# Start-up loads on two queues, own blocks for six operand splits, and a longer period for the second stream of weight sums in a fused attention and feed-forward layer

## The chip, the cores and the metric

The kernel runs on one core of a Trainium2 chip, as one launch. The metric is the device time of one execution in microseconds (us); lower is better. The times of before are those of three runs: 1481.43, 1481.87 and 1482.26 us.

## The reference, cut to what matters

One layer on x of 256 rows and 2048 columns, in float32, with a memory `mem` of the same shape:

```python
proj = rms_norm(x, g_mix) @ w_in               # heads of three attentions, and 3 x 2048 gate columns
mk, mv = split(rms_norm(mem, g_mem) @ w_mem_kv, 2)
o_fox, o_sb, o_mem = forgetting(...), stick_breaking(...), memory(...)
g = sigmoid(gates + b_gate)
merged = g[0] * (o_fox @ w_br_fox) + g[1] * (o_sb @ w_br_sb) + g[2] * (o_mem @ w_br_mem)
x = x + merged @ w_out
u_gate, u_val = split(causal_conv3(rms_norm(x, g_ffn) @ w_up) + conv_b, 2)
return x + (silu(u_gate) * u_val) @ w_down
```

In the stick-breaking attention (six heads of width 128), with z the scaled scores, the weight of key j for query i is exp(log_sigmoid(z) + R), where R is the sum of log(1 - sigmoid(z)) over the keys between j and i. That sum is made by a matrix product with a triangle of ones.

## The kernel before, in words

Every large product is float32 work done in three passes. A float32 operand is split into a rounded part `hi` and a rest `lo`: `piece` (lines 134 to 145) loads a piece of a weight (1024 columns per partition) into one of four `raw` buffers with a DMA on SyncE's queue (SP), ScalarE (ACT) copies it to `hi` (line 140), VectorE (DVE) subtracts to get `lo` (line 141). TensorE (PE) then does hi times hi, lo times hi, hi times lo in `passes` (lines 147 to 153), three matmuls of 512 columns each. There are four `raw`, four `hi` and four `lo` buffers.

The work goes through PE in this order: the key and value product of the memory (`kv`, 16 steps of k, lines 450 to 485), the projections with w_in (mq, f0 to f4, s0 to s4, and twelve gate products g, in four column groups n), the three branch products b of each n, the output product o, the up product u with its convolution, and the down product.

**The start.** `memres` holds `mem`. The helper `mem_piece(k, n)` loads n column blocks of 128 from block k on, always on SP's queue (line 275). Block 0 is asked for first; then `kvw` block 0 as two halves of 512 columns, mem block 1, and in the loop over k the weight of k + 1 as one piece of 1024 columns (`kv_weights`) and mem blocks 2k + 2 and 2k + 3 for k under 7; from k = 7 on the x columns (`x_piece`, line 426). PE transposes mem blocks (line 192), ACT and DVE scale and split them into `memT` (lines 178 and 181), and `kv_part` (line 438) runs the two column halves of the step. Small constants (gains, tap rows of the convolution, a bias; lines 305 to 326) are issued on SP as well. They are a generator that advances once per step from k = 2 on, and they are not pinned: a scheduler that lays out each engine's instructions ahead of the run may move them. Instructions that go through `pin` or `in_order` keep their order among each other. Each DMA counts on one of eight completion semaphores in turn, so that a DMA waits at its issuing queue until the one eight places before it (of both queues) has landed.

**The blocks.** `block` takes one of 14 buffers of 1024 columns (`bp`); heads, gates and transposed products live in them. Small work goes through the pool `sm`; its tag `junk` has two buffers of 512 columns.

**The stick-breaking heads.** `sb_head` (line 651) is a generator; two heads are in work at a time, and each `tick()` (one per two k of a product) takes one step of each. A head computes log(1 - sigmoid) into `l1`, masks it with GpSimd (POOL, line 646), splits it into two parts `ls[0]` (ACT, line 669) and `ls[1]` (DVE, line 670), and multiplies these with the triangle (line 674) and the ones (line 676). Both parts are `junk` tiles, so one head's two parts fill both buffers until its matmuls have read them.

**The weight sums.** For 22 pairs of w_down's row blocks the down product uses sums of weights made beforehand. `weight_sums(staging, period)` takes 44 half pairs from one shared list. For each it loads 512 KB (two DMAs on SP, line 232), adds on DVE (lines 239 to 241), and five ticks later stores 512 KB (`kept`, line 244). A new half starts every `period` ticks. The first stream starts at the end of mq, has period 6, and stages in one buffer of its own (`pre`), so that its next load waits for the landing of its last store. The second starts at n = 1 with period 8 and stages in blocks. Both draw from the list until it is empty; all must be done by the end of the o product.

Of the kernel before, what the change touches and what calls it, by code (L numbers as in the profile page):

```python
# [10 lines left out]
F32R = mybir.dt.float32r  # L11
# [4 lines left out]
P = 128  # L16
# [24 lines left out]
def hybrid_block(  # L41
# [25 lines left out]
    nc = tc.nc  # L67
# [5 lines left out]
    sm = ctx.enter_context(tc.tile_pool(name="sm", bufs=4))  # L73
# [6 lines left out]
    def bank(name):  # L80
        return pp.tile([P, 512], F32, tag="bank", name=name)
# [14 lines left out]
    def later(gen):  # L96
        waiting.append(gen)

    background = []
# [28 lines left out]
    def pin(ins):  # L128

        if pinned[0]:  # L130
            tc.keep_in_program_order(ins)


    def piece(src, a, n, name):
        raw = wp.tile([P, PIECE], F32, tag="raw", name=f"raw_{name}")
        hi = wp.tile([P, PIECE], F32R, tag="hi", bufs=SBUFS, name=f"hi_{name}")
        lo = wp.tile([P, PIECE], F32R, tag="lo", bufs=SBUFS, name=f"lo_{name}")
        m = a * n
        pin(nc.sync.dma_start(raw[:, :m].rearrange("p (a n) -> p a n", a=a), src))
        pin(nc.scalar.copy(hi[:, :m], raw[:, :m]))  # L140
        pin(nc.vector.tensor_tensor(lo[:, :m], raw[:, :m], hi[:, :m].bitcast(F32), ALU.subtract))  # L141
        return (
            hi[:, :m].rearrange("p (a n) -> p a n", a=a),
            lo[:, :m].rearrange("p (a n) -> p a n", a=a),
        )
# [76 lines left out]
    def weight_sums(staging, period):  # L222

        while halves:
            nb, pr, h = halves.popleft()
            if h == 0:
                sums_of[nb, pr] = dram.tile([P, 4, 512], F32, tag=f"kept_{nb}_{pr}", name=f"kept_{nb}_{pr}")
            w = staging(f"pre_{nb}_{pr}_{h}").rearrange("p (i c) -> p i c", i=4)
            n0 = nb * PIECE + h * 256
            for n in range(2):  # L230
                in_order(
                    nc.sync.dma_start(
                        w.rearrange("p (k n) c -> p k n c", k=2)[:, :, n],
                        dv[:, 2 * pr : 2 * pr + 2, n0 + n * 512 : n0 + n * 512 + 256],
                    )
                )

            both = w[:, 1:2].to_broadcast([P, 2, 256])
            in_order(nc.vector.tensor_tensor(w[:, 0:2], w[:, 0:4:3], both, ALU.add))
            in_order(nc.vector.tensor_tensor(w[:, T2], w[:, T1], w[:, T2], ALU.add))  # L240
            in_order(nc.vector.tensor_tensor(w[:, T4], w[:, T2], w[:, T4], ALU.add))
            for _ in range(5):
                yield
            in_order(nc.sync.dma_start(sums_of[nb, pr][:, :, h * 256 : (h + 1) * 256], w))
            for _ in range(period - 5):
                yield
# [6 lines left out]
    mv = mem[0].rearrange("(t p) d -> p t d", p=P)  # L253
    memres = xt_pool.tile([P, NT, D], F32, tag="xt", name="memres")
# [16 lines left out]

    tiles_of = lambda g: g.rearrange("(k p) -> k p", p=P)

    def mem_piece(k, n=2):
        pin(nc.sync.dma_start(memres[:, :, k * P : (k + n) * P], mv[:, :, k * P : (k + n) * P]))

    rows_mem = load_rows(nc.scalar, [(tiles_of(g_mem[0]), KT)], "mem")
    mem_piece(0, 1)
    bfor = cst.tile([P, N_FOX], F32, name="bfor")

    ones_r = cst.tile([P, P], F32R, name="ones_r")
# [87 lines left out]
    def block(name, dt=F32):  # L369
        return bp.tile([P, 1024], dt, tag="blk", name=name)  # L370
# [64 lines left out]
    kv = [[bank(f"kv_{c}_{t}") for t in range(NT)] for c in range(2)]  # L435
    kvw = w_mem_kv[0].rearrange("(k p) n -> p k n", p=P)
# [7 lines left out]
    w = {}  # L444

    def kv_weights(k):
        wh, wl = piece(kvw[:, k : k + 1, :], 1, 1024, f"kv{k}")
        w[k] = [(wh[:, 0, c * 512 : (c + 1) * 512], wl[:, 0, c * 512 : (c + 1) * 512]) for c in range(2)]

    h0 = [piece(kvw[:, :1, :512], 1, 512, "kv0_0")]  # L450
    to_mT(0, 1)
    keep_busy(3)
    h0.append(piece(kvw[:, :1, 512:], 1, 512, "kv0_1"))
    w[0] = [(h[:, 0], l[:, 0]) for h, l in h0]
    mem_piece(1, 1)
    xT = None
    squares = deque((j, t) for j in range(4) for t in range(NT))
    for k in range(KT):
        if k == 0:
            kv_part(0, 0, *w[0][0])  # L460
            to_mT(1, 1)
        if k + 1 < KT:
            kv_weights(k + 1)
        if k < 7:
            mem_piece(2 * k + 2)
        elif k < 15:
            x_piece(2 * (k - 7))
        if k == 2:
            later(constants())
        if k > 0:  # L470
            kv_part(k, 0, *w[k][0])
        if 0 < k < 8:
            to_mT(2 * k)
        elif k > 8:
            transposed(xT, xres, gmix, 2 * (k - 9), "xT")
        kv_part(k, 1, *w.pop(k)[1])
        for _ in range(0 if k < 3 else 1 if k < 8 else 3):
            if squares:
                j, t = squares.popleft()
                square_part(ssm, memres, j, "m", (t,))  # L480
        if k == 8:
            row_rstd(rstd_m, ssm, "m")
            xT = k_tiles("xT")
        tick()
# [156 lines left out]
    W3 = 3 * P  # L641
# [9 lines left out]
    def sb_head(h):  # L651
        yield from until("s0", "s1", "s2")
        q, k = qs[h // 4][:, h % 4], qs[(N_SB + h) // 4][:, (N_SB + h) % 4]
        b = block(f"sb_{h}")
        lb, l1 = b[:, :W3], b[:, W3 : 2 * W3]
        Z = bank(f"z_{h}")
        z = Z[:, :W3]
        nc.tensor.matmul(z[:, :S], lhsT=k[:, :P], rhs=q, start=True, stop=True)
        nc.tensor.matmul(z[:, S:], lhsT=k[:, P:], rhs=q[:, P:], start=True, stop=True)
        nc.scalar.activation(lb, z, AF.Abs)  # L660
        nc.scalar.activation(lb, lb, AF.Exp, scale=-1.0)
        nc.scalar.activation(lb, lb, AF.Ln, bias=1.0)
        nc.vector.scalar_tensor_tensor(lb, z, 0.0, lb, ALU.min, ALU.subtract)
        nc.vector.tensor_tensor(l1, lb, z, ALU.subtract)
        diagonal(l1)
        yield 2

        ls = [sm.tile([P, 512], F32R, tag="junk", bufs=2, name=f"ls_{h}_{i}")[:, :W3] for i in range(2)]
        nc.scalar.copy(ls[0], l1)
        nc.vector.tensor_tensor(ls[1], l1, ls[0].bitcast(F32), ALU.subtract)  # L670
        yield 1
        r = bank(f"r_{h}")
        for i in range(2):
            nc.tensor.matmul(r[:, :W3], lhsT=after_r, rhs=ls[i], start=i == 0, stop=False)
        for i in range(2):
            nc.tensor.matmul(r[:, P:S], lhsT=ones_r, rhs=ls[i][:, S:], start=False, stop=i == 1)
        nc.vector.tensor_tensor(lb, lb, r[:, :W3], ALU.add)
        nc.scalar.activation(lb, lb, AF.Exp)
        diagonal(lb)
        yield 2  # L680
        yield from until("vs0", "vs1")
        weighted(lb, vs, h, N_FOX + h, Z)
# [31 lines left out]

    for n in range(4):
        if n == 1:
            background.append(weight_sums(block, 8))
        n0 = n * 512
        gate = []
        for b in range(3):  # L720
            bg = gp.tile([P, 512], F32, tag="bg", name=f"bg_{n}_{b}")
            nc.sync.dma_start(bg, b_gate[0, b, n0 : n0 + 512].partition_broadcast(P))
            ps = proj(C_GATE + b * D + n0, 512, f"g{n}_{b}")
            g = rows_of(block(f"g_{n}_{b}"))
            for t in range(NT):
                nc.vector.scalar_tensor_tensor(g[:, t], ps[t], rstd[:, t : t + 1], bg, ALU.mult, ALU.add)
            if n > 0:
                nc.scalar.activation(g, g, AF.Sigmoid)
            gate.append(g)
        if n == 0:  # L730
            finish()
            for g in gate:
                in_order(nc.scalar.activation(g, g, AF.Sigmoid))
        acc = rows_of(block(f"acc_{n}"))
        for i, (w, k0, nk, b) in enumerate(branches):
            ps = product(lambda k: oT[:, k0 + k], w[0], nk, n0, 512, f"b{n}_{b}")
            for t in range(NT):
                g = gate[b]
                if i == 0:
                    nc.vector.tensor_tensor(acc[:, t], g[:, t], ps[t], ALU.mult)  # L740
                else:
                    nc.vector.tensor_tensor(g[:, t], g[:, t], ps[t], ALU.mult)
                    nc.vector.tensor_tensor(acc[:, t], acc[:, t], g[:, t], ALU.add)
        later(merged_T(acc, n))
# [22 lines left out]
    for n in range(4):  # L767
        c = slice(n * 512, (n + 1) * 512)
# [48 lines left out]
    for f0 in range(0, FT, 4):  # L817
        for s in range(2):
            ps = [bank(f"u{f0 + i}_{s}") for i in range(4)]
            c0 = s * D_FF + f0 * P  # L820
            for k in range(0, KT, 2):
                hi, lo = piece(upv[:, k : k + 2, c0 : c0 + 512], 2, 512, f"u{f0}_{s}_{k}")
                for j in range(2):
                    first, last = k + j == 0, k + j == KT - 1
                    for i in range(4):
                        c = slice(i * P, (i + 1) * P)
# [167 lines left out]
    for nb, plan in enumerate(plans):  # L994
# [17 lines left out]
        for t in range(NT):  # L1012
            for n in range(2):
                c = n0 + n * 512
                o = xres[:, t, c : c + 512]
                nc.vector.tensor_tensor(o, o, X[t][n], ALU.add)
                if (nb, t, n) == (1, 1, 1):
                    nc.scalar.dma_start(ov[:, t, c : c + 256], o[:, :256])
                    c, o = c + 256, o[:, 256:]
# [35 lines left out]
```

## Time and profile before

| what | value |
|---|---|
| median of 3 runs | 1481.87 us (1481.43 to 1482.26) |
| the profiled execution's own time | 1483.94 us |
| its span, first to last instruction | 1482.2 us |
| DVE busy | 1073.0 us (72%) |
| ACT busy | 801.8 us (54%) |
| HBM read, written | 320.60 MB, 25.17 MB |
| granted TensorE clock | 0.999 |

The span leaves 1.74 us of the profiled execution's own time outside it. The profile's busy time of PE is the time in which some matmul is under way; matmuls overlap, and their ends are modelled. Waits are named by the engine that waited, the line, and whom it waited for. In a timeline row stand the start, the length, the engine (SPq and ACTq are the queues that issue DMAs), the line, the operation, the tiles written and read, their shape, a count, and in brackets the idle time of the engine before it with what ended it.

### The profile page before, as it was taken

Reading aid. Unit: us, or ns where it says so; the run is one execution under the profiler, and the core shown is the slowest. Engines: PE = TensorE matmul, PEld = TensorE weight load, DVE = VectorE, ACT = ScalarE, POOL = GpSimd, SP = SyncE. Lnnn points to the kernel's source line nnn. Section 1 sums busy time; section 2 is a strip of 40 time slices with the busy share of each in tenths; the row PEclk is TensorE's granted clock in tenths of the full one; section 3 lists DMA queues with packets and bytes.
Section 4 is the critical chain, followed back from the end, with each engine's and each line's share of the span. In section 5 each row is a group of like instructions: output and inputs, shape, how many; then the busy total and the mean of one; then the engine's idle time right before and its main releaser. Section 6 shows DMA issues by size and latency. Waiting matters only on the chain.

```text
span 1482.2 us, 20334 instructions
## 1 busy us (share of the span) xinstructions
PE 1473.9 (99%) x7394; PEld 1248.5 (84%) x7394; DVE 1073.0 (72%) x1604; ACT 801.8 (54%) x1141; POOL 17.9 (1%) x46
## 2 busy tenths in 40 slices
PE   9999999999999999999999999999999999999999
PEld 6888888888888887888888888888888888888887
DVE  5777676666765867666557787787787787997877
ACT  6755454464544343444456565565565565674664
POOL 0000000011000000000000000000000000000000
PEclk9999999999999999999999999999999999999999
DMA  9686687587788989975556566556556656798796
GB/s 306 197 276 208 189 290 222 172 274 233 260 288 282 322 290 306 313 252 191 184 180 207 187 187 198 185 185 198 188 186 195 189 184 203 242 318 280 248 338 216
DMA packets 198308, 347.12 MB, mean 234 GB/s; under 512 B 12458, under 2 KB 66622, under 8 KB 198206
## 3 DMA queue, kind: packets, MB, share of 16 engines
q1 hardware_dynamic: 196878, 343.71, 71.4%
q10 hardware_dynamic: 1328, 2.11, 0.4%
q8 instruction: 58, 0.95, 0.2%
q14 instruction: 44, 0.36, 0.1%
HBM read 320.60 MB, written 25.17 MB: 233 GB/s over the span
## 4 chain that ended last, share of the span: by engine, by line
PE 95%; DMA 3%; DVE 1%; ACT 0%; SPq 0%; issue 0%; DVEq 0%; ACTq 0%
PE u L827 22%; PE u L828 11%; PE g L151 5%; PE g L152 5%; PE g L153 5%; PE x L913 4%; PE x L914 4%; PE x L912 4%; PE s L151 2%; PE s L153 2%; PE s L152 2%; PE f L151 2%; PE f L153 2%; PE f L152 2%; PE o L153 2%; PE o L151 2%
## 5 line engine op out<-in xcount | busy, mean ns | idle before, releaser
L827 PE MATMUL u<-hT,hi_u 128*128 128x512 f32 x1232 | 428.4, 391 | 0.0
L828 PE MATMUL u<-hT,lo_u 128*128 128x256 f32 x1232 | 345.0, 280 | 0.0
L141 DVE TENSOR_TENSOR lo_u<-raw_u,hi_u 128x1024 fp32r<-128x1024 f32 x176 | 215.2, 1222 | 115.2 <-ACT hi_u L140 115.2
L827 PEld LDWEIGHTS u<-hT,hi_u 128*128 128x128 f32 x1232 | 230.4, 187 | 50.5
L140 ACT CAST hi_u<-raw_u 128x1024 fp32r<-128x1024 f32 x176 | 184.8, 1050 | 139.4 <-PE u L827 111.2
L828 PEld LDWEIGHTS u<-hT,lo_u 128*128 128x128 f32 x1232 | 232.8, 189 | 0.0
L140 ACT CAST hi_g<-raw_g 128x1024 fp32r<-128x1024 f32 x96 | 100.8, 1052 | 141.1 <-PE g L152 67.4
L141 DVE TENSOR_TENSOR lo_g<-raw_g,hi_g 128x1024 fp32r<-128x1024 f32 x96 | 116.0, 1221 | 57.5 <-ACT hi_g L140 54.5
L151 PE MATMUL g<-hi_g,xT 128*128 128x512 f32 x336 | 132.0, 393 | 0.0
L153 PE MATMUL g<-lo_g,xT 128*128 128x512 f32 x336 | 131.0, 390 | 0.2 <-DVE lo_g L141 0.2
L152 PE MATMUL g<-hi_g,xT 128*128 128x512 f32 x336 | 130.8, 389 | 0.0
L908 DVE TENSOR_TENSOR lo_d<-raw_d,hi_d 128x1024 fp32r<-128x1024 f32 x88 | 106.6, 1221 | 20.9 <-ACT hi_d L907 17.9
L907 ACT CAST hi_d<-raw_d 128x1024 fp32r<-128x1024 f32 x88 | 92.1, 1054 | 45.6 <-PE x L913 21.7
L914 PE MATMUL x<-lo_d,aT 128*128 128x512 f32 (+1 forms) x202 | 78.4, 388 | 0.0
L913 PE MATMUL x<-hi_d,aT 128*128 128x512 f32 (+1 forms) x202 | 78.4, 388 | 0.0
L912 PE MATMUL x<-hi_d,aT 128*128 128x512 f32 (+1 forms) x202 | 78.4, 388 | 0.0
L153 PEld LDWEIGHTS g<-lo_g,xT 128*128 128x128 f32 x336 | 63.0, 188 | 14.1 <-DVE lo_g L141 0.6
L152 PEld LDWEIGHTS g<-hi_g,xT 128*128 128x128 f32 x336 | 63.1, 188 | 12.8
L151 PEld LDWEIGHTS g<-hi_g,xT 128*128 128x128 f32 x336 | 63.1, 188 | 12.7
L140 ACT CAST hi_f<-raw_f 128x1024 fp32r<-128x1024 f32 (+1 forms) x40 | 38.6, 967 | 51.5 <-PE f L152 46.5
L141 DVE TENSOR_TENSOR lo_o<-raw_o,hi_o 128x1024 fp32r<-128x1024 f32 x32 | 39.2, 1224 | 36.8 <-ACT hi_o L140 32.3
L141 DVE TENSOR_TENSOR lo_f<-raw_f,hi_f 128x1024 fp32r<-128x1024 f32 (+1 forms) x40 | 44.6, 1118 | 27.9 <-ACT hi_f L140 26.3
(365 smaller groups left out, 2941.2 us busy)
## 6 DMA issues: line engine op xcount, KB each, us to landing
raw_u<-in_w_up_dram SPq DMA_DIRECT2D x176, 512.0 KB, 3.4
raw_g<-in_w_in_dram SPq DMA_DIRECT2D x96, 512.0 KB, 5.5
raw_d<-in_w_down_dram SPq DMA_DIRECT2D x66, 512.0 KB, 5.8
pre<-in_w_down_dram SPq DMA_DIRECT2D x88, 256.0 KB, 3.6
kept<-pre SPq DMA_DIRECT2D x44, 512.0 KB, 5.1
raw_f<-in_w_in_dram SPq DMA_DIRECT2D x32, 512.0 KB, 4.4
raw_s<-in_w_in_dram SPq DMA_DIRECT2D x32, 512.0 KB, 4.3
raw_o<-in_w_out_dram SPq DMA_DIRECT2D x32, 512.0 KB, 4.2
```

Of the source, the lines that this page charges most:

```text
L140: pin(nc.scalar.copy(hi[:, :m], raw[:, :m]))
L141: pin(nc.vector.tensor_tensor(lo[:, :m], raw[:, :m], hi[:, :m].bitcast(F32), ALU.subtract))
L151: pin(nc.tensor.matmul(o, lhsT=xh, rhs=wh, start=first, stop=False))
L152: pin(nc.tensor.matmul(o, lhsT=xl, rhs=wh, start=False, stop=False))
L153: pin(nc.tensor.matmul(o, lhsT=xh, rhs=wl, start=False, stop=last))
L827: nc.tensor.matmul(ps[i], lhsT=hi[:, j, c], rhs=hT(k + j), start=first, stop=False)
L828: nc.tensor.matmul(ps[i][:, :S], lhsT=lo[:, j, c], rhs=hT(k + j)[:, :S], start=False, stop=last)
L907: nc.scalar.copy(hi[:, :n], src)
L908: nc.vector.tensor_tensor(lo[:, :n], src, hi[:, :n].bitcast(F32), ALU.subtract)
L912: nc.tensor.matmul(o, lhsT=ah, rhs=w[0], start=first, stop=False)
L913: nc.tensor.matmul(o, lhsT=al, rhs=w[0], start=False, stop=False)
L914: nc.tensor.matmul(o, lhsT=ah, rhs=w[1], start=False, stop=last)
```

## The change

`mem_piece` gets a queue as argument. Blocks 1 (one block) and 2, 3 (one piece of two) are asked for on ACT's queue right after block 0; the call for block 1 behind the first weights is gone, and the loop's call is now under `0 < k < 7`. The `elif` behind it is unchanged. The second weight (k = 1) is loaded and split as two halves of 512 columns, each with buffers of its own. The two parts of a stick-breaking split are now the halves of one block `ls_h`. The second stream of weight sums has period 18.

```diff
-    def mem_piece(k, n=2):
-        pin(nc.sync.dma_start(memres[:, :, k * P : (k + n) * P], mv[:, :, k * P : (k + n) * P]))
+    def mem_piece(k, n=2, q=nc.sync):
+        pin(q.dma_start(memres[:, :, k * P : (k + n) * P], mv[:, :, k * P : (k + n) * P]))
 
     rows_mem = load_rows(nc.scalar, [(tiles_of(g_mem[0]), KT)], "mem")
     mem_piece(0, 1)
+    mem_piece(1, 1, nc.scalar)
+    mem_piece(2, 2, nc.scalar)
...
     def kv_weights(k):
-        wh, wl = piece(kvw[:, k : k + 1, :], 1, 1024, f"kv{k}")
-        w[k] = [(wh[:, 0, c * 512 : (c + 1) * 512], wl[:, 0, c * 512 : (c + 1) * 512]) for c in range(2)]
+        if k == 1:
+            h = [piece(kvw[:, k : k + 1, c * 512 : (c + 1) * 512], 1, 512, f"kv{k}_{c}") for c in range(2)]
+            w[k] = [(hi[:, 0], lo[:, 0]) for hi, lo in h]
+        else:
+            hi, lo = piece(kvw[:, k : k + 1, :], 1, 1024, f"kv{k}")
+            w[k] = [(hi[:, 0, c * 512 : (c + 1) * 512], lo[:, 0, c * 512 : (c + 1) * 512]) for c in range(2)]
...
-    mem_piece(1, 1)
...
-        if k < 7:
+        if 0 < k < 7:
             mem_piece(2 * k + 2)
         elif k < 15:
             x_piece(2 * (k - 7))
...
-        ls = [sm.tile([P, 512], F32R, tag="junk", bufs=2, name=f"ls_{h}_{i}")[:, :W3] for i in range(2)]
+        parts_of = block(f"ls_{h}", F32R).rearrange("p (i c) -> p i c", i=2)
+        ls = [parts_of[:, i, :W3] for i in range(2)]
...
-            background.append(weight_sums(block, 8))
+            background.append(weight_sums(block, 18))
```

The order of the built program shows what this moves. At k = 0 the `elif` now holds, and `x_piece(-14)` is issued: it loads x's columns 256 to 511, which `x_piece(2)` loads again at k = 8. On SP's queue the first five DMAs are mem block 0, the two halves of weight 0 and the two halves of weight 1; then come this x piece and all nine small constant loads (lines 307, four of 310, 313, 319, 321 and 323), and only then weight 2, mem blocks 4 and 5, weight 3, and so on. Before, weight 2 was the seventh DMA on SP, with two mem pieces and no constant between it and weight 0's second half but weight 1; the constants stood further back. On PE, ACT and DVE the order of the start is the same but for the halves. In the heads 2 to 5, the two heads' splits and triangle products now stand next to each other; of the 44 half pairs, 7 are staged in blocks and 11 were.

## The prediction

> **What bounds the kernel now.** I read the page first, then what PE waited for, then the start and the two other places of these waits in the timeline.
>
> ```profile
> span 1482.2 us, 20334 instructions
> PE 1473.9 (99%) x7394; PEld 1248.5 (84%) x7394; DVE 1073.0 (72%) x1604; ACT 801.8 (54%) x1141; POOL 17.9 (1%) x46
> ```
>
> TensorE is busy 99% of the span. The change takes no matmul away, so it can win only PE's idle time, 1482.2 - 1473.9 = 8.3 us, and what overlapping ends hide. All of PE's waits but that ahead of its first matmul (in total, times, longest, in us):
>
> ```profile
> PE b L153 <- DVE lo_b L141: 1.0, 1, 1.0
> PE r L674 <- ACT ls L669: 0.8, 1, 0.8
> PE kv L151 <- ACT hi_kv L140: 0.7, 1, 0.7
> PE kv L153 <- DVE lo_kv L141: 0.5, 1, 0.5
> PE g L153 <- DVE lo_g L141: 0.2, 1, 0.2
> ```
>
> They belong to the three places that the change touches: kv is weight 1 at the start, r the stick-breaking parts, b and g the stage with both streams of weight sums. An idle time understates the loss, since a matmul is shown about 0.39 long while the next follows 0.23 later (the rows at 362.49 and 362.71 below): each stop costs 0.16 us more than its idle time. So kv loses 0.75 + 0.53 + 2 x 0.16 = 1.6 us, r at least 0.8 + 0.16 = 1.0, b and g 1.0 + 0.2 + 2 x 0.16 = 1.5.
>
> **Part 1, the start.** Timeline of before; the column of interest is the start, in us:
>
> ```profile
> 2.27 0.43 SPq L275 DMA_DIRECT2D memres<-in_mem_dram  x1
> 2.75 0.47 SPq L139 DMA_DIRECT2D raw_kv<-in_w_mem_kv_dram  x1
> 3.73 0.47 SPq L139 DMA_DIRECT2D raw_kv<-in_w_mem_kv_dram  x1
> 4.72 0.75 SPq L307 DMA_DIRECT2D rows_mix<-in_g_mix_dram  x1
> ...
> 8.57 1.05 ACT L140 CAST hi_kv<-raw_kv 128x1024 fp32r<-128x1024 f32 x1 [0.51 <-DMA raw_kv<-in_w_mem_kv_dram]
> 9.65 1.23 DVE L141 TENSOR_TENSOR lo_kv<-raw_kv,hi_kv 128x1024 fp32r<-128x1024 f32 x1 [1.07 <-ACT hi_kv L140]
> 9.67 0.50 PE L151 MATMUL kv<-hi_kv,memT 128*128 128x512 f32 x1 [0.75 <-ACT hi_kv L140]
> 10.54 1.05 ACT L140 CAST hi_kv<-raw_kv 128x1024 fp32r<-128x1024 f32 x1 [0.93 <-DMA raw_kv<-in_w_mem_kv_dram]
> 10.93 0.50 PE L153 MATMUL kv<-lo_kv,memT 128*128 128x512 f32 x1 [0.53 <-DVE lo_kv L141]
> 13.47 0.87 DVE L181 SCALAR_TENSOR_TENSOR memT<-mT,gmem_c,memT 128x256 fp32r<-128x256 f32 x2 [0.62 <-ACT memT L178]
> 14.02 0.48 PE L152 MATMUL kv<-hi_kv,memT 128*128 128x512 f32 x1
> ```
>
> Weight 1 is asked for at 2.75 and cast at 8.57; PE stops for the cast and again for the rest. With halves, cast and subtraction take about half of 1.05 and 1.23, and nothing is asked for between weight 0 and weight 1, so I expect both stops gone: -1.6 us.
>
> But weight 2, asked for at 3.73 before, goes behind the extra x piece and nine constants. They issue on SP for 0.43 (the length of a mem piece's row above, of the same size as the x piece) and
>
> ```profile
> 5.52 0.43 SPq L310 DMA_DIRECT2D rows_mix<-in_g_q_fox_dram  x1
> 5.99 0.30 SPq L310 DMA_DIRECT2D rows_mix<-in_g_k_fox_dram  x1
> ...
> 11.19 0.25 SPq L310 DMA_DIRECT2D rows_mix<-in_g_q_mem_dram  x1
> 11.48 0.25 SPq L310 DMA_DIRECT2D rows_mix<-in_g_k_mem_dram  x1
> 14.39 0.33 SPq L313 DMA_DIRECT2D rows_mix<-in_g_ffn_dram  x1
> 19.81 0.47 SPq L319 DMA_DIRECT2D bfor<-in_b_forget_dram  x1
> 20.32 0.39 SPq L321 DMA_DIRECT2D taps_rows<-in_conv_w_dram  x1
> 20.75 0.40 SPq L323 DMA_DIRECT2D taps_rows<-in_conv_b_dram  x1
> ```
>
> 0.75 + 0.43 + 0.30 + 0.25 + 0.25 + 0.33 + 0.47 + 0.39 + 0.40 = 3.57. Five DMAs 0.48 apart put the x piece at 3.2; with 4.0 of issue and ten gaps of 0.05, weight 2 is asked for at 7.7 at the earliest. It will be later: eight semaphores go round, so line 319 waits until the second half of weight 1 has landed, line 321 until the x piece has, line 323 until the first constant has. The window of 5 to 10 us shows how fast data comes (last column, GB/s):
>
> ```profile
> 5.00:10.00 5.00, 4.25 (x17) 2.84 (x16) 2.28 (x5) 2.15 (x4) 0.00 (x0) 1.00 0.92 312
> ```
>
> Weight 1 took 5.8 us from issue to cast; for its second half, issued at 2.7, I take 5.3, so 8.0; the x piece's 256 KB come 0.8 later at 312 GB/s, so 8.8 or 9.0. Then line 321 at 9.0, 323 at 9.4, weight 2 at 9.8. From issue to landing:
>
> ```profile
> DMA to landing us min/median/max: 4.2/5.1/6.8
> DMA to landing us min/median/max: 3.5/5.9/8.0
> ```
>
> (the first is raw_kv, amid mem and x pieces; the second raw_d, pieces of the same form in the down product.) Behind the small constants the queue is nearly empty, so I stay by the low end, 3.5: weight 2 lands at 13.3, against 10.54 before. In the programs' order its cast stands before the memT casts of blocks 2 and 3 on ACT, its subtraction before theirs on DVE. So PE's second pass of step 2 follows the landing by 1.05 (cast), 1.23 (subtraction), 0.44 (half of memT's 0.87) and four steps of 0.03 between them: 2.84. It stood at 14.02. PE is then late by 13.3 + 2.84 - 14.02 = **+2.1 us**, and this takes the place of the 1.6 won, it isn't added to it: that gain would show in full only if weight 2 landed by 14.02 - 1.6 - 2.84 = 9.6. Bounds: 7.7 + 3.5 = 11.2 gives 0.0, and 10.5 + 5.1 = 15.6 gives +4.4. Behind it mem blocks 4, 5 and weight 3 follow 0.4 and 0.9 later on SP, ahead of what PE wants of them; the steps are bound by PE there (no wait of PE in a kv step but those of weight 1), so the delay neither grows nor shrinks. The x piece's second copy overwrites equal data before it is read.
>
> The two mem pieces on ACT's queue are issued before ACT's first cast and cost it nothing; sharing the DMA engines may bring weight 0 and PE's first matmul up to 0.5 later (384 KB take 1.2 at 312 GB/s, and I give weight 0's packets less than half of the delay). The wait for weight 2 covers that; without the wait it costs 0.5. [...]
>
> **Part 2, own blocks.** The timeline at heads 2, 3 (the first two rows) and 4, 5:
>
> ```profile
> 333.03 0.40 PE L153 MATMUL g<-lo_g,xT_rest 128*128 128x512 f32 x1
> 333.47 0.44 PE L674 MATMUL r<-ls,after_r 128*128 128x384 f32 x1
> ...
> 350.77 0.50 ACT L669 CAST ls<-sb 128x384 fp32r<-128x384 f32 x1
> ...
> 360.73 0.51 PE L674 MATMUL r<-ls,after_r 128*128 128x384 f32 x2
> ...
> 362.20 0.44 PE L674 MATMUL r<-ls,after_r 128*128 128x384 f32 x1 [0.80 <-ACT ls L669]
> 362.49 0.39 PE L151 MATMUL g<-hi_g,xT 128*128 128x512 f32 x1
> 362.71 0.39 PE L152 MATMUL g<-hi_g,xT 128*128 128x512 f32 x1
> ```
>
> Head 5's first part can be written only when head 4's matmuls have read the two junk buffers: 1.0 lost at 362.20, and for heads 2 and 3, 0.44 - 0.23 = 0.2 at 333.47. Head 4's own was written at 350.77, 10 us before PE read it. With own blocks head 5's is written right behind it in ACT's and DVE's order, so that most of these 10 us are its cover; the 0.5 us copy that now stands ahead of a gate's cast fits in it. Blocks: each `ls` follows a tile whose last reader is long done in the built program's addresses (qk_fox, y of s0 and s1, sb_0, sb_1), so no new wait. I take **-1.3**, with some 0.1 for the switches to and fro; bounds -1.6 and -0.9.
>
> **Part 3, the second stream.** Windows of 100 and 50 us; the last two columns are the DMA engines' share and GB/s:
>
> ```profile
> 500.00:600.00 100.00, 98.77 (x441) 80.98 (x440) 69.96 (x90) 41.24 (x41) 0.00 (x0) 1.00 0.92 302
> 700.00:750.00 50.00, 50.00 (x234) 41.66 (x233) 28.17 (x32) 25.11 (x39) 0.00 (x0) 1.00 0.57 189
> ```
>
> Counting ticks, before starts 1/6 + 1/8 = 0.29 halves a tick, after 1/6 + 1/18 = 0.22. The sums' traffic, 302 - 189 = 113 GB/s, falls to 86, so the stage moves 275. The longer of PE's two stops shows in the chain of waits,
>
> ```profile
> 573.89 1.23 DVE lo_b L141
> ```
>
> a piece that comes late behind loads and stores of both streams. With 7 halves in blocks for 11, such meetings are rarer: I take three quarters of the 1.5, **-1.2**; bounds -1.6 and +0.5 (a new meeting). The work not done there, 30 ticks of it, goes into the output product, which moves 189 GB/s and has DVE busy 28 of 50 us; the additions fit in there. The list is empty at tick 226 of 240, so nothing reaches the up product.
>
> **Sum.** +2.1 - 1.3 - 1.2 = -0.4 us. On the profiled execution: 1483.94 to 1483.5. It lies 2.07 above the median, 1.74 of that outside its span; the same step from the median 1481.87 gives **1481.5**.
>
> **The rivals.**
>
> (a) SP doesn't wait. If the second half of weight 1 and the x piece land before SP comes to lines 319 and 321, weight 2 is asked for at 7.7 and lands at 11.2: 0.0 - 1.3 - 1.2 = -2.5, **1479.4**; with parts 2 and 3 at their bounds -3.2, 1478.7. For it: half a weight is half the bytes of weight 1's 5.8 us. Against: at 312 GB/s the 1.8 MB up to the x piece's end take 5.9 us from the first packet on, landing not counted.
>
> (b) Slower. Landings keep the slow pace of the first 10 us: weight 2 asked for at 10.5 takes raw_kv's longest, 6.8, and lands at 17.3, so 17.3 + 2.84 - 14.02 = +6.1; with -2.5 from the rest +3.6, **1485.5**. The total is above before once weight 2 lands after 13.7, above by 0.2% after 16.6. For it: weight 1's 5.8. Against: nothing large is left in the queue by then.
>
> (c) Part 3 doesn't do what it says. SP still stops at the one buffer's store,
>
> ```profile
> SPq L232 <- DMA kept<-pre: 67.5, 29, 5.6
> ```
>
> and the stops only move: +2.1 - 1.3 + 0 = +0.8, **1482.7**.
>
> **How the numbers follow.** Forecast 0.56, (a) 0.17, (b) 0.13, (c) 0.14. What a measurement of this kernel can tell from no change is about 0.2%, 3.0 us: below 1478.9 is faster, above 1484.8 slower. Forecast and (c) lie within, with their bounds; half of (a) is faster, as its parts 2 and 3 fall, and (b) is slower: faster 0.09, same 0.78, slower 0.13. The range takes in (a) with its lowest sum, and above the upper bound of the start with a third of part 3's gain (+4.4 - 1.3 - 0.4 = +2.7): 1478.7 to 1484.6. It leaves out (b) and little else.
>
> **What would show it.** Weight 2's cast at about 13.3 and its SP row at about 9.8, behind line 323; PE idle before step 2, none at step 1; the r rows without a stop; no lo_b or lo_g wait of PE between 540 and 580. A cast of weight 2 before 11 refutes part 1; a wait of PE in the output product refutes part 3.

## The result and the profile after

| | before | after |
|---|---|---|
| median of 17 runs each, one chip | 1483.57 us (1481.23 to 1486.47) | 1486.72 us (1483.34 to 1487.98) |
| the traced execution, its span | 1483.94, 1482.2 us | 1484.46, 1482.7 us |

The ratio is 1.0021, with a 95% interval of [1.0013, 1.0028]: slower by 0.2%. The before of these runs lies 1.70 us above the three runs that the prediction started from. The page of after:

```profile
span 1482.7 us, 20340 instructions
PE 1475.3 (99%) x7394; PEld 1251.4 (84%) x7394; DVE 1075.9 (73%) x1605; ACT 802.8 (54%) x1142; POOL 16.4 (1%) x46
```

It tells nothing: 0.5 us more span, and PE 1.4 us busier with the same 7394 matmuls. What PE waited for (total, times, longest) does:

```profile
PE kv L151 <- ACT memT L178: 1.8, 2, 1.1
PE spare L90 <- DVE qscale L295: 1.2, 1, 1.2
PE kv L152 <- DVE memT L181: 0.8, 1, 0.8
```

The waits r, b and g are gone; what is left, but for the one ahead of PE's first matmul, belongs to the start. Where the time went can be summed: for each matmul the distance to the next one's start, less the usual distance for its line and shape.

| lost by PE, us | before | after | change |
|---|---|---|---|
| 0 to 20 us, the start | 3.06 | 7.07 | +4.0 |
| 320 to 380, the stick-breaking parts | 1.79 | 0.46 | -1.3 |
| 540 to 580, both streams of sums | 1.84 | -0.06 | -1.9 |
| elsewhere | 4.40 | 4.12 | -0.3 |

So the traced +0.5 is a loss of 4.0 at the start against gains of 3.5. First the start, in the timeline of after (start and length in us; the constants' lines stand two further on than in the kernel before, so its 307, 319, 321 and 323 are 309, 321, 323 and 325 here):

```profile
3.22 0.43 SPq L429 DMA_DIRECT2D xres<-in_x_dram  x1
5.44 0.34 SPq L309 DMA_DIRECT2D rows_mix<-in_g_mix_dram  x1
5.44 0.62 ACT L140 CAST hi_kv<-raw_kv 128x512 fp32r<-128x512 f32 x1 [3.37 <-DMA raw_kv<-in_w_mem_kv_dram]
...
9.53 0.40 SPq L325 DMA_DIRECT2D taps_rows<-in_conv_b_dram  x1
10.04 0.35 SPq L139 DMA_DIRECT2D raw_kv<-in_w_mem_kv_dram  x1
...
15.32 1.05 ACT L140 CAST hi_kv<-raw_kv 128x1024 fp32r<-128x1024 f32 x1 [3.63 <-DMA raw_kv<-in_w_mem_kv_dram]
16.80 0.50 PE L151 MATMUL kv<-hi_kv,memT 128*128 128x512 f32 x1 [0.68 <-ACT memT L178]
18.08 0.50 PE L152 MATMUL kv<-hi_kv,memT 128*128 128x512 f32 x1 [0.79 <-DVE memT L181]
```

Weight 2 is asked for at 10.04, behind the x piece and the nine constants, and cast at 15.32, 5.28 later; PE's second pass of step 2 starts at 18.08, where it stood at 14.02. The same stretch as SP sees it (its waits up to 11 us):

```profile
SPq L309 <- DMA raw_kv<-in_w_mem_kv_dram: 1.8, 1, 1.8
SPq L312 <- DMA raw_kv<-in_w_mem_kv_dram: 1.2, 2, 1.0
...
SPq L323 <- DMA xres<-in_x_dram: 0.2, 1, 0.2
```

Of the 10 us SP stood 3.2 us, each time with a constant at its head that had to wait for an earlier DMA's landing, and weight 2 behind it. Of these, 3.0 stood at the gain rows, which waited for pieces of weights 0 and 1.

PE's named waits at the start grew only from 1.2 to 2.6 us, while its loss grew by 4.0. The rest is in its pitch. Rows of after before and behind 13 us:

```profile
10.39 0.63 PE L152 MATMUL kv<-hi_kv,memT 128*128 128x512 f32 x1
10.81 0.63 PE L153 MATMUL kv<-lo_kv,memT 128*128 128x512 f32 x1
...
13.43 0.39 PE L151 MATMUL kv<-hi_kv,memT 128*128 128x512 f32 x1
13.66 0.40 PE L152 MATMUL kv<-hi_kv,memT 128*128 128x512 f32 x1
```

Until 13 us the matmuls start 0.42 apart and are 0.63 long, then 0.23 and 0.39: PE ran at half its clock (in the second trace of after, below, they start 0.43 apart where 0.50 is recorded). In this execution it cost nothing of its own, for at full clock PE would have stood that much longer for weight 2, as it does in that second trace, 3.84. But the mean granted clock of the 17 runs of after does not look like the traced one's 1.000: in 11 runs it is 0.997 or 0.998, and these take 1486.1 to 1488.0 us; in six it is 0.999 or 1.0, and these take 1483.3 to 1485.8.

The third part, as the windows of after show it (DMA share and GB/s last):

```profile
500.00:600.00 100.00, 100.00 (x448) 82.80 (x447) 68.95 (x82) 42.43 (x42) 0.00 (x0) 1.00 0.89 286
700.00:750.00 50.00, 50.00 (x234) 41.67 (x233) 29.07 (x37) 25.05 (x38) 0.00 (x0) 1.00 0.64 209
```

PE is busy all of the 100 us, where it was 98.77; the traffic went from 302 to 286 GB/s, and what was moved out of the stage turned up in the output product, 209 for 189, at no cost to PE.

### The profile page after: what moved, and what is told of

Read it like the earlier page. It is cut to its first block, busy times and chain, and to the rows that moved or that the text cites. A ratio compares the mean times of both kernels' runs of the same rounds, so it can differ in the third digit from the quotient of the medians.

```text
span 1482.7 us, 20340 instructions
## 1 busy us (share of the span) xinstructions
PE 1475.3 (99%) x7394; PEld 1251.4 (84%) x7394; DVE 1075.9 (73%) x1605; ACT 802.8 (54%) x1142; POOL 16.4 (1%) x46
## 4 chain that ended last, share of the span: by engine, by line
PE 99%; DMA 1%; DVE 0%; issue 0%; ACT 0%; SPq 0%; DVEq 0%
PE u L833 22%; PE u L834 11%; PE g L151 6%; PE g L153 6%; PE g L152 6%; PE x L918 4%; PE x L919 4%; PE x L920 4%; PE s L151 2%; PE s L153 2%; PE s L152 2%; PE f L151 2%; PE f L153 2%; PE f L152 2%; PE o L153 2%; PE o L152 2%
## 5 line engine op out<-in xcount | busy, mean ns | idle before, releaser
L141 DVE TENSOR_TENSOR lo_s<-raw_s,hi_s 128x1024 fp32r<-128x1024 f32 (+1 forms) x40 | 44.9, 1123 | 23.5 <-ACT hi_s L140 20.8
```

## The experiments

Three questions: which part loses (theory A: the start, by SP's order; B: parts 2 and 3; C: ScalarE's queue or the pace of transfers), why the median lies above the traced run (D: PE's clock falls back behind the start's waits; E, F: another cause), and why weight 2 took 5.28 us from issue to cast (G, H, I, J). Each ratio is to the kernel before on the same chip.

### Parts 2 and 3 alone

```diff
-        ls = [sm.tile([P, 512], F32R, tag="junk", ...)[:, :W3] for i in range(2)]
+        parts_of = block(f"ls_{h}", F32R).rearrange("p (i c) -> p i c", i=2)
+        ls = [parts_of[:, i, :W3] for i in range(2)]
...
-            background.append(weight_sums(block, 8))
+            background.append(weight_sums(block, 18))
```

> The kernel before with own blocks for the splits and period 18, its start left as it was. Theory A (the start alone makes the loss; the other two parts give what the trace of after shows): no wait of PE at r, b or g, second pass of step 2 near 14.0 us, span 3.2 us below that of before, timed ratio about 0.998. Theory B (the loss of the timed runs comes from the sums that moved into the output product, or from the blocks): not below before, ratio 1.000 or more.

Measured: 1480.40 us (1479.68 to 1481.15, 11 runs), ratio 0.9984 [0.9975, 0.9992], span 1478.5. PE's losses: 2.94 at the start, 0.39 and -0.06 at the two other places. Theory B falls: these parts win 3.3 of the 3.7 us of span. The timed runs give less, 2.4 us (1.2 to 3.7); what is lost between 540 and 580 us differs from trace to trace, 1.84 in before and 1.2 in the next run, which has the same two streams.

### The start alone

The kernel before with the edits of `mem_piece`, `kv_weights` and the loop only.

> Only the start of the change; junk tiles and period 8 as before. Theory A: weight 2 asked for near 10.0 and cast near 15.3 as in after, second pass of step 2 near 18.1, span 4 us above before, timed ratio 1.003 to 1.005, with PE's granted clock below 0.999 in most runs, as in after. Theory B: ratio at most 1.001.

Measured: 1489.57 us (1487.65 to 1491.95, 6 runs), ratio 1.0051 [1.0038, 1.0064], span 1486.6. Weight 2 is asked for at 10.27 and cast at 15.39; PE loses 7.14 in the first 20 us, as in after. The traced run has a clock of 1.0, the other five 0.997 or 0.998. The loss is the start's, and the low clock comes with it, though not in every run.

### The start with SP's order mended

```diff
-        nc.sync.dma_start(rows[:KT], tiles_of(g_mix[0]))
+        pin(nc.sync.dma_start(rows[:KT], tiles_of(g_mix[0])))
...
-        elif k < 15:
+        elif 7 <= k < 15:
             x_piece(2 * (k - 7))
...
-            nc.sync.dma_start(bg, b_gate[0, b, n0 : n0 + 512].partition_broadcast(P))
+            load_bg = nc.sync.dma_start(bg, b_gate[0, b, n0 : n0 + 512].partition_broadcast(P))
+            if n == 0:
+                in_order(load_bg)
```

The other constants are pinned in the same way. No x piece at k = 0; constants and gate biases stay behind the weights.

> After, with the x piece at k = 0 left out (its columns are loaded at k = 8 in any case) and the small constants and the first three gate biases held behind in SP's order, so that weight 2 is the sixth DMA on SP; it still has to wait for the first raw buffer to come free (6.8 us in after). Theory A: weight 2 asked for near 7.0, cast by 12.0, second pass of step 2 near 15, span about 2 us below before. Theory C (not SP's order but the pace of the transfers is what delays weight 2: mem pieces on ACT's queue, first touches of the weight): weight 2 takes as long to come as the 5.3 us it took in after plus the wait behind mem pieces, is cast after 13.5 and the start still costs 3 us or more.

Measured: 1480.65 us (1479.74 to 1481.18, 11 runs), ratio 0.9985 [0.9977, 0.9994], span 1478.5, clocks 0.999 to 1.0. Weight 2's rows:

```profile
1.30 5.02 SPq L139 DMA_DIRECT2D raw_kv<-in_w_mem_kv_dram  x5
6.37 0.44 SPq L275 DMA_DIRECT2D memres<-in_mem_dram  x1
7.69 0.33 SPq L139 DMA_DIRECT2D raw_kv<-in_w_mem_kv_dram  x1
...
11.19 1.05 ACT L140 CAST hi_kv<-raw_kv 128x1024 fp32r<-128x1024 f32 x1 [1.58 <-DMA raw_kv<-in_w_mem_kv_dram]
```

Five weight DMAs are grouped in the first row; the fifth is weight 2, at 6.0. The row at 7.69 is weight 3's. PE loses 3.01 in the first 20 us, as before: with the order mended the start of the change neither wins nor loses, and the whole loss is SP's order. Theory A holds.

### Weight 1 in one piece

```diff
-        if k == 1:
+        if k < 0:
...
-        elif k < 15:
+        elif 7 <= k < 15:
```

> After, with the x piece at k = 0 left out and weight 1 in one piece again, so that weight 2 has a free raw buffer and stands fifth on SP, ahead of the constants by the built order. Theory A: weight 2 asked for near 2.8, second pass of step 2 within 1.5 us of before's 14.0, span 2 us below before. Theory C: weight 0 is still cast near 5.4 (4.0 before) since block 1 to 3 of mem come by ACT's queue, and the start is later than before by that 1.4 us or more.

Measured: 1481.81 us (1480.92 to 1491.22, 11 runs, the second highest 1482.2), ratio 1.0001 [0.9989, 1.0013], span 1480.0. The constants may slip in here too, but one piece less of weight 1 leaves a `raw` buffer for weight 2, which goes out at 2.74, ahead of them. PE runs at half clock until 11.0 and loses 4.34 at the start. This fits the following account of the hole in SP's order: weights 0 and 1 in halves take all four `raw` buffers, weight 2 must wait for weight 0's split, and the scheduler fills the time with loads that nothing holds back.

### The x piece or the constants

After with constants and gate biases pinned as above, but the x piece of k = 0 left ahead of weight 2 (`elif k < 15`).

> The changed kernel with the constants' loads and the first three gate biases held behind the weights in SP's order, but with the x piece of k = 0 still ahead of weight 2. Theory A with the constants as the cause: weight 2 is asked for as soon as its buffer is free, at about 7.7, the x piece's 256 KB cost it at most 0.8, it is cast by 12.0, and the time lies within 1 us of that of the kernel with neither (1480.65). If the x piece is the cause: weight 2 cast at 14 or later, and 1483 or more.

Measured: 1480.51 us (1479.99 to 1481.34, 10 runs), ratio 0.9987 [0.9978, 0.9996]. SP's order around weight 2, and the last of three casts:

```profile
3.22 0.43 SPq L429 DMA_DIRECT2D xres<-in_x_dram  x1
5.85 0.33 SPq L139 DMA_DIRECT2D raw_kv<-in_w_mem_kv_dram  x1
...
9.61 2.16 ACT L140 CAST hi_kv<-raw_kv 128x512 fp32r<-128x512 f32 x3
```

Weight 2 goes out at 5.85, earlier than the 7.7 that I expected, which is the row of weight 3. Its cast ends at 11.77, so it began at 10.72. The x piece is harmless (1480.65 without it); it was the constants (the gate biases, pinned with them, went out behind weight 2 in the changed kernel too).

### Halves on SP alone

After with the pins and the guard of above, and all mem pieces back on SP:

```diff
-    mem_piece(1, 1, nc.scalar)
-    mem_piece(2, 2, nc.scalar)
...
+    mem_piece(1, 1)
...
-        if 0 < k < 7:
+        if k < 7:
```

> The changed kernel with weight 1's halves kept, but all mem pieces on SP as in the kernel before (block 1 behind the halves of weight 0, blocks 2 and 3 behind weight 1), no x piece at k = 0, and the constants' loads and the first three gate biases held behind the weights in SP's order. Theory A (the start's loss is SP's order alone): weight 2 asked for at 5 to 7.7 and cast by 11.2, weight 0 cast at about 4.0 as before, no wait of TensorE for weight 1, 1.0 to 1.6 us less lost in the first 20 us than before's 3.06; with the 3.2 of the other parts 1478.0 to 1479.5 beside a before of 1482.25, ratio 0.9970 to 0.9982. If ScalarE's queue is itself a gain, weight 1's halves come late here and the start loses as much as before: 1479.5 to 1480.7.

Measured: 1479.67 us (1478.83 to 1480.29, 11 runs), ratio 0.9980 [0.9971, 0.9989], span 1477.8. Weight 0 and weight 2:

```profile
3.94 0.62 ACT L140 CAST hi_kv<-raw_kv 128x512 fp32r<-128x512 f32 x1 [1.86 <-DMA raw_kv<-in_w_mem_kv_dram]
...
5.31 0.33 SPq L139 DMA_DIRECT2D raw_kv<-in_w_mem_kv_dram  x1
...
10.51 1.05 ACT L140 CAST hi_kv<-raw_kv 128x1024 fp32r<-128x1024 f32 x1 [1.46 <-DMA raw_kv<-in_w_mem_kv_dram]
```

Weight 0 comes at 3.94; in the ten traces with mem pieces on ACT's queue and weight 1 in halves it came at 4.5 to 5.4. PE loses 2.35 at the start, 0.7 less than before, less than the 1.0 to 1.6 expected. This is the fastest version tried, ahead of both kernels; against parts 2 and 3 alone, in other runs, its ratio is not told apart.

### The changed kernel again

> The changed kernel once more, for a second trace. If its granted clock is 0.997 to 0.998, as in 11 of its 17 runs so far: theory D expects a stretch of matmuls 0.43 apart instead of 0.23 behind the stops of the first 20 us, some 3 to 4 us lost by it, and a span of about 1485.5; rival E expects the slow stretch elsewhere, beyond 30 us. If its clock is 1.0, the span is about 1482.7 and nothing is told apart.

Measured: 1486.19 us, span 1484.4, clock 0.997. The windows of this run (first column behind the stretch's length: PE; third from the end: granted clock):

```profile
12.00:13.00 1.00, 0.99 (x5) 0.46 (x3) 0.00 (x0) 0.00 (x0) 0.00 (x0) 1.00 0.90 280
13.00:14.00 1.00, 0.00 (x0) 0.00 (x0) 0.00 (x0) 0.00 (x0) 0.00 (x0) 1.00 0.85 258
14.00:15.00 1.00, 0.00 (x0) 0.00 (x0) 0.00 (x0) 0.00 (x0) 0.00 (x0) 1.00 0.83 305
15.00:16.00 1.00, 0.00 (x0) 0.00 (x0) 0.00 (x0) 0.64 (x1) 0.00 (x0) 0.54 1.04 349
16.00:17.00 1.00, 0.17 (x1) 0.17 (x1) 0.56 (x1) 1.00 (x3) 0.00 (x0) 0.50 0.99 325
...
20.00:21.00 1.00, 1.00 (x5) 0.80 (x4) 0.00 (x0) 0.00 (x0) 0.00 (x0) 0.50 1.06 390
21.00:22.00 1.00, 1.00 (x5) 0.89 (x4) 0.00 (x0) 0.50 (x2) 0.00 (x0) 0.55 1.04 407
22.00:23.00 1.00, 1.00 (x6) 0.80 (x5) 0.62 (x2) 1.00 (x2) 0.00 (x0) 1.00 1.07 412
```

Here PE was at full clock by 4.8 us, did step 1 fast (matmuls 0.23 apart), and so stood idle from 12.99 on (its last matmul starts at 12.59 and is 0.40 long) for 3.8 us, waiting for the same weight 2, cast at 15.36. The clock fell at 15.08 (0.54 is half for 0.92 of that window) and came back at 21.90: 0.92 + 5 + 0.90 = 6.82 us at half. The rows there:

```profile
16.83 0.79 PE L151 MATMUL kv<-hi_kv,memT 128*128 128x512 f32 x1 [3.84 <-ACT memT L178]
...
19.13 0.63 PE L151 MATMUL kv<-hi_kv,memT 128*128 128x512 f32 x1
19.56 0.63 PE L152 MATMUL kv<-hi_kv,memT 128*128 128x512 f32 x1
```

PE loses 9.32 up to 40 us, against 7.60 in the first trace of after: 1.7 us, which is the difference of the spans. Theory D's stretch is there, behind the stops of the start; the price is 1.7, not the 3 to 4 expected.

### Idle-time matmuls in the waits

`keep_busy(n)` issues n matmuls of 384 columns whose result nobody reads.

```diff
-    keep_busy(3)
+    keep_busy(7)
...
+        if k == 2:
+            keep_busy(12)
         if k > 0:
             kv_part(k, 0, *w[k][0])
```

> The changed kernel with more idle-time matmuls on TensorE: seven instead of three sets ahead of weight 0's second half, and twelve sets ahead of kv step 2. They compute nothing that is used and stand where TensorE would wait. Theory D (in most runs of the changed kernel TensorE's clock falls back to half for some microseconds because of its waits at the start, which the traced run, where it stayed at 1.0 behind them, does not show): the granted clock is 0.999 or above in nearly all runs, against 0.997 to 0.998 in 11 of 17 of the changed kernel, and the median is about 3 us below that of the changed kernel, 1483.5 to 1484.5, while weight 2 still lands at about 15.3 and the traced span stays within 1 us of 1482.7. Rival E (the low clocks have another cause, later in the run, or are of the chip that it ran on): the clocks stay spread as in the changed kernel and the median lies at 1486 to 1488.

Measured: 1486.02 us (1483.60 to 1486.49, 11 runs), ratio 1.0021 [1.0012, 1.0030]. The clocks rose to 0.999 or above in ten of the runs and 0.998 in one, but seven lie at 1486.0 to 1486.5 and four at 1483.6 to 1484.7. As to the median this was a miss for D, and it left F open. The traced run was of the lower group: 1.8 us of the wait stayed open (1.03 and 0.79). The same kernel traced again:

> The kernel with seven and twelve sets of idle-time matmuls once more, for a trace of its upper group (7 of 11 runs at 1486.0 to 1486.5, granted clock 0.998 to 0.999). Theory D: a stretch at half clock of 2 to 4 us behind the rest of the wait for weight 2. Rival F: clock full from 6 us on, and the time lost elsewhere. A run of the lower group (1483.6 to 1484.7) tells nothing.

Measured: 1486.09 us, span 1484.4 against 1481.9, clock 0.999. Its windows:

```profile
15.00:16.00 1.00, 0.00 (x0) 0.00 (x0) 0.00 (x0) 0.57 (x1) 0.00 (x0) 1.00 1.00 373
...
19.00:20.00 1.00, 1.00 (x5) 0.70 (x4) 0.70 (x1) 0.00 (x0) 0.00 (x0) 0.54 1.04 390
20.00:21.00 1.00, 1.00 (x5) 0.92 (x4) 0.00 (x0) 0.17 (x1) 0.00 (x0) 0.50 1.05 398
21.00:22.00 1.00, 1.00 (x4) 0.79 (x3) 0.30 (x1) 1.00 (x3) 0.00 (x0) 0.50 1.05 419
22.00:23.00 1.00, 1.00 (x5) 0.82 (x4) 0.94 (x3) 0.60 (x1) 0.00 (x0) 0.75 1.04 393
```

Half clock from 19.08 to 22.50, 3.42 us, behind stops of 2.0 and 0.8 us: worth 1.7 us, as PE was busy all that time. Weight 2 was also cast 0.96 later (15.43 for 14.47), which makes the rest of the 2.5 us. So both D and F are in this run of the group. Then the whole wait filled, with `keep_busy(22)` for `keep_busy(12)`:

> As the kernel with seven and twelve sets of idle-time matmuls, but 22 sets ahead of kv step 2, so that TensorE's whole wait for weight 2 is filled (the traced wait of the changed kernel at a full clock was 3.8 us; with twelve sets 1.9 of it was left open). Theory D (the part of the wait that is left open still lets the clock fall back in some runs): clocks 1.0 or 0.999 throughout, the upper group of runs at 1486.0 to 1486.5 goes, median 1483.5 to 1484.5. Rival F (the upper group is not the clock's, but a later landing of weight 2 or something behind the start): the two groups stay as with twelve sets, with a median near 1486.

Measured: 1484.55 us (1483.97 to 1484.99, 11 runs), ratio 1.0015 [1.0006, 1.0024], all clocks 0.999 or 1.0. The upper group is gone, though weight 2 was cast as late as 15.91 in the traced run. D holds; the matmuls that fill the wait give none of the 4.0 us back.

### What is behind weight 2, and ahead of it

```diff
+        if k == 1:
+            pin(nc.scalar.copy(memres[:, 0, 4 * P : 4 * P + 1], w[2][0][0][:, :1].bitcast(F32)))
         if 0 < k < 7:
             mem_piece(2 * k + 2)
```

with the gate biases pinned; mem piece 4 and all behind it on SP now wait for weight 2's cast.

> The changed kernel with nothing issued on SP behind weight 2 until it has been cast: a one-element copy from the cast weight into the block that mem piece 4 then overwrites makes this piece's DMA, and all behind it in SP's order, wait for the cast; the first three gate biases are held behind the weights. The mem pieces and weights 3 on come some 4 us later for it, so only the landing of weight 2 is read, not the time. Theory G (weight 2's 5.28 us from issue to cast, where 3.5 was forecast, are shared with the mem pieces and weights that SP issues behind it from 10.4 on): 512 KB at the 300 to 370 GB/s of the windows take 1.4 to 1.7 us, and it is cast 3.0 to 3.9 us after its issue. Rival H (a piece of this form takes 5 us from issue to landing whatever is behind it, or the constants ahead of it hold it up): 4.8 us or more.

Measured, in one run whose time (1486.42 us) tells nothing, as all behind weight 2 is held up: asked for at 10.44, cast at 14.98, so 4.54 us, between the two bands. The windows say why (DMA share of 16 engines, GB/s):

```profile
11.00:12.00 1.00, 1.00 (x6) 0.83 (x5) 0.60 (x1) 0.00 (x0) 0.00 (x0) 1.00 0.88 249
12.00:13.00 1.00, 1.00 (x9) 0.82 (x7) 0.00 (x0) 0.00 (x0) 0.00 (x0) 1.00 0.92 332
13.00:14.00 1.00, 1.00 (x7) 0.83 (x6) 0.00 (x0) 0.00 (x0) 0.00 (x0) 1.00 0.12 49
14.00:15.00 1.00, 0.59 (x3) 0.16 (x1) 0.00 (x0) 0.01 (x1) 0.00 (x0) 1.00 0.03 12
```

From 13 on a tail: 0.12 x 16 is two engines, 0.03 x 16 half of one, with nothing else under way. Then the three constants of lines 321 to 325 pinned behind as well:

> The kernel with nothing issued behind weight 2, and with the last three constants (the forget bias, 128 packets of 24 bytes, and the two of the taps, 352 packets of 512 bytes) held behind the weights as well; the six small gain rows and the x piece stay ahead of it. In the run with all nine ahead, weight 2 was cast 4.54 us after its issue, though 113 of its 128 packets had gone by 2.5 us after it: the last ones went one after another until 14.4, with 0.12 and 0.03 of the 16 DMA engines busy. Theory I (these few engines were still at the small constants when weight 2 came): without the three, weight 2 is asked for at 8.9 to 9.3 and cast 3.0 to 3.7 us later, with no tail of single packets. Rival J (the tail is the transfer's own, or the gain rows'): 4.2 us or more.

Measured, again in one run (1483.83 us): asked for at 8.53, cast at 12.07, so 3.54 us.

```profile
8.53 0.36 SPq L139 DMA_DIRECT2D raw_kv<-in_w_mem_kv_dram  x1
...
12.07 1.05 ACT L140 CAST hi_kv<-raw_kv 128x1024 fp32r<-128x1024 f32 x1 [2.31 <-DMA raw_kv<-in_w_mem_kv_dram]
```

This is as theory I has it, from one trace, in which weight 2 was also asked for 1.9 us earlier; which of the three constants counts is not shown. By these two traces weight 2's 5.28 us would be 3.54 of its own, 1.00 behind the three small constants and 0.74 shared with what comes behind it. The split is rough. In the six traces that have SP's order of the changed kernel, weight 2 took 4.74 to 6.00 us from issue to cast. So 3.54 is clear of them, by 1.2 us, and the tail speaks for the constants; the 0.74 is not told apart from the scatter.

Why small loads ahead should hold weight 2 up is not shown: which engine carried a packet the trace does not tell.

## Why the prediction was wrong

- **What bounds the kernel** held: all gains and losses are PE's stops, and they add up to the span within 0.3 us.
- **Part 1, SP's order**, was right, and the issue time too: 9.8 forecast, 10.04 traced. The forecast had no wait ahead of line 319 and the trace has 3.0 us of them, at the gain rows; they did not count, since the last wait, for the x piece, ended at 9.16 for a forecast 9.0.
- **Part 1, weight 2's landing**, is the step that failed first: 3.5 us were taken, with the reason that "behind the small constants the queue is nearly empty", and 5.28 traced. The queue was nearly empty in bytes (10 GB/s from 9 to 10 us, 0.06 of the engines); but the small constants stood just ahead of it, and SP at once issued the delayed pieces behind it. With neither, 3.54 was measured; how the difference splits between the two is open. The row of raw_kv itself, median 5.1, would have been right, and stood in the prediction as the upper bound. From the cast to PE's second pass it was 2.76 for 2.84. Summed: +2.1 + 0.24 + 1.78 - 0.08 = +4.0.
- **Part 1, weight 0** came 1.4 us later than before, not up to 0.5 (0.7 in the runs with weight 0 at 4.7). The wait for weight 2 did cover it.
- **"The delay neither grows nor shrinks"** failed: no rival held that a stop also costs clock. Behind a wait that in one trace of after was 3.8 us long, PE ran at half clock for 6.8 us, 1.7 us more lost. That 11 of 17 runs have the low clock puts the median into that group; the 1.7 itself is from one trace.
- **Part 2**: -1.3 forecast, -1.3 traced. **Part 3**: -1.2 forecast, -1.9 traced, no new meeting; the traffic of the stage fell to 286 GB/s, not 275, and that was enough.
- **The sum**: -0.4 forecast for the traced execution, +0.5 traced. From 1481.5 to 1486.72 are 5.2 us: 1.7 is before's own median on this chip, 1.9 weight 2, 1.7 the clock, -0.7 part 3 and -0.3 elsewhere; some 0.9 is not accounted for, and part 3's share differs between traces as said above. The difference that the ratio's interval allows, 1.9 to 4.2 us, takes in the 2.2 by which the second trace of after lies above that of before.
- **The rivals**: (b) came nearest: weight 2 was cast 1.6 us behind its turning point of 13.7, though not at 17.3. Its reason, landings that keep the slow pace of the first 10 us, isn't what the runs show: with nothing behind it and only the gain rows just ahead, weight 2 took 3.54. (a) fell with SP's waits, (c) with part 3's gain.

## What to carry to other kernels

When a change takes one more buffer or DMA slot at a tight place, look at what the scheduler puts into the hole: loads that nothing orders will go ahead of the transfer that the critical engine waits for, and pinning them behind it turned +0.21% into -0.13%. Price a transfer by the row of the same tile in the same company, its median, and not by the best row of a quieter stage. Near the start, add to a stop of PE the chance that the clock falls with it, and take several traces: one showed a clock of 1.000 where most runs had 0.997 or 0.998.

## What the runs showed of the hardware

- **The clock's fall.** Three traces caught one near the start: PE idle from 12.99, half clock from 15.08; stops of 2.0 and 0.8 us, half clock from 19.08; and, in the run that holds back what is behind weight 2, stops of 2.08 and 0.55 us from 14.60 and 17.18, half clock from 17.55 to 20.96 (granted clock 0.77, 0.50, 0.50, 0.52 in the windows from 17 to 21). The stretches are 6.82 = 2 x 3.41, 3.42 and 3.41 us. The length of a stop does not decide alone. The run with the start alone had the same stops as the second of these, and its clock stayed full:

```profile
16.86 0.50 PE L151 MATMUL kv<-hi_kv,memT 128*128 128x512 f32 x1 [2.07 <-ACT memT L178]
...
18.15 0.50 PE L152 MATMUL kv<-hi_kv,memT 128*128 128x512 f32 x1 [0.79 <-DVE memT L181]
```

What tells them apart may be where the stops lie; this is an estimate from these traces. The clock rose near 4.8 us in the first of the three and near 10.7 in the third, by the length and pitch of the matmuls, and fell 10.3 and 6.8 us later, about three and two times the 3.41 of the stretches at half clock. In the 3.41 us ahead of each fall PE stood 2.09, 2.01 and 2.45 us in all. Counted in slots of 3.41 us from its rise near 9.7, the run with the start alone has a slot's end at 16.52, which cuts the stop of 2.07 in two; the first part, 1.73, is the most that PE stood in such a slot near the start, from full clock and without a fall. The 0.999 of the trace of before is such a fall behind PE's last matmul and no loss: that one ends at 1478.5, and the clock falls at 1480.6 (granted 0.80 from 1480 to 1481, 0.50 behind).
- **The warm-up.** Full clock came at 6.0 us in the trace of before and at 13.0 in that of after, at 4.4 to 11.0 in others. In the windows of after ahead of 13 us the column of the granted clock shows 1.00 all the same, and only the pitch of the matmuls, 0.42 for 0.23, tells it.
- **Two queues.** With the mem pieces on ACT's queue, weight 0 was cast at 4.5 to 5.4 us, 0.5 to 1.5 later than with them on SP behind it (3.94).
